# Two-layer hybrid encoder trunk: the recurrence's query and forget-gate projections computed in the product form, with the affine of the second layer's gates on ScalarE

## The chip, the cores and the metric

The kernel runs on one core of one Trainium2 chip. The metric is the device time of one execution in microseconds (us), the median over several runs. For the kernel before it is 1301.94 us (three runs, 1301.85 to 1302.33).

## The reference, cut to what matters

The program is two layers of an encoder on 256 tokens of width 1024, all in float32. Each layer projects the residual stream x once (`w_in`) and feeds three mixers with it: pooling, attention, and a bidirectional gated recurrence (HGRN2) with 8 heads of 128. The change touches only what goes into the recurrence:

```python
q = jax.nn.silu(heads(q_raw))                       # q_raw = x @ w_in[:, query columns]
def forget(raw, lb):                                # raw   = x @ w_in[:, gate columns], two directions
    z = heads(raw)
    f = lb + (1.0 - lb) * jax.nn.sigmoid(z)
    return (1.0 - lb) * jax.nn.sigmoid(-z), jnp.log(f)
```

`lb` is zero in layer 0 and one value per channel in layer 1. From f, (1-f) and q the recurrence forms running products over chunks of the tokens, then small matrix products. The three mixers are projected, gated and added, an output projection and a layer norm follow, then a SwiGLU FFN and a second layer norm.

## The kernel before, in words

All weights are streamed once, as 212 chunks of 1 MB. For each chunk a DMA brings `raw` (line 207), ScalarE rounds it to float32r, `whi` (line 225), and VectorE subtracts, `wlo` = raw - whi (line 228). x is kept in the same two parts, xh and xl, side by side in one tile `xx` (hi, then lo, 256 tokens each). A product is then hi*hi + hi*lo + lo*hi, three float32r products that add up to nearly float32. `raw`, `whi` and `wlo` have three buffers each.

There are three ways to multiply with a chunk:

- `gemm_cols` (lines 360 to 367): the chunk holds 256 output columns in 8 contraction tiles. For each of two halves m and each k there are three matmuls of 256 tokens (lines 356 to 358): whi*xh, whi*xl, wlo*xh, 48 matmuls per chunk. Both halves fit into one PSUM bank.
- `gemm_wide` (lines 369 to 381), the product form: for each m and k one matmul of whi with all 512 columns of `xx`, which gives hi*hi in the left half of a bank and hi*lo in the right half, and one matmul of wlo with xh, 32 matmuls per chunk. Each m needs a bank of its own, and the two halves of the bank must be added afterwards. `joined` (lines 383 to 387) does that: per m a copy of the left half by ScalarE (line 386), then VectorE adds the right half to it (line 387).
- `tok_part` (lines 398 to 408, matmuls at line 407), with tokens as output rows, in 24 matmuls per chunk.

The FFN, the pooling projection and three of the attention chunks use the product form already.

The work of one layer goes in this order: the recurrence's value chunks (v), then four head pairs, hp0 to hp3 here. Each head pair takes three chunks: the query (called q below), the forward gate (f0) and the backward gate (f1). Behind hp0 come four chunks for the output gate, behind hp1 four and behind hp3 two for attention's values. Then come the attention's query and key chunks and the rest.

The order on ScalarE, VectorE and TensorE is fixed while the program is written. At the end of each chunk's matmuls `step_end` (line 337) emits, in this order: the recurrence's "background" work on VectorE (scans, reciprocals, products, lines 524 to 577) up to a budget written in the code, then the eviction of the chunk just multiplied, and then `split_chunk`, which emits the `wlo` subtraction that the previous step left over and the `whi` of a new chunk. So when chunk n has been multiplied, the `wlo` that is emitted belongs to chunk n+2, and the `whi` to chunk n+3. Each engine runs its list in order.

The evictions before: for q, ScalarE takes the sigmoid from PSUM (line 935) and VectorE multiplies it with PSUM (line 936). For a gate chunk, ScalarE takes sigmoid(z) and sigmoid(-z) from PSUM (lines 945 and 948), and VectorE sets two border columns to 1 (line 946). In layer 1 four more VectorE instructions of 256 columns follow, the affine with `omlb` = 1-lb and `lb` (lines 952 and 954).

`gbank` hands out four PSUM banks in turn. A step of `gemm_cols` takes one, a step of `gemm_wide` two.

Of the kernel before, what the change touches and what calls it, by code (L numbers as in the profile page):

```python
# [11 lines left out]
AF = mybir.ActivationFunctionType  # L12
ALU = mybir.AluOpType
# [4 lines left out]
S = 256  # L18
# [60 lines left out]
def trunk(ctx: ExitStack, tc: tile.TileContext, x, p, w_in, pool_w, pool_scale, w_branch_a,  # L79
# [3 lines left out]
    V, A, PE, G = nc.vector, nc.scalar, nc.tensor, nc.gpsimd  # L83
# [39 lines left out]
    def gbank():  # L123
        return psg.tile([P, 512], F32, tag="g", name="g")
# [127 lines left out]
    def use_chunk():  # L252
        if pos["use"] == pos["split"] - 1:
            flush()
        i = pos["use"]
        pos["use"] += 1
        return split.pop(i)
# [79 lines left out]
    def step_end(then=None, budget=3000, banks=1, need=0, keep=2):  # L337


        background(budget)  # L340
        if then is not None:
            pend.append((then, banks, need))
        while pend:
            fn, _, n = pend[0]
            if held[0] + n > 10 and sum(e[1] for e in pend) <= keep:
                break
            pend.pop(0)
            if n:
                room(n)
            fn()  # L350
        split_chunk()
# [8 lines left out]
    def gemm_cols(w, act, ps, nk=8, m0=0, nm=2):  # L360
        for m in range(nm):
            if m == 1:
                amid()
            for k in range(nk):
                ms = slice((m0 + m) * P, (m0 + m + 1) * P)
                mm3(ps[:, m * S:(m + 1) * S], (w[0][:, k, ms], w[1][:, k, ms]),
                    act(k), k == 0, k == nk - 1)
# [15 lines left out]
    def joined(ps, dst):  # L383

        for m in range(2):
            A.activation(out=dst[:, m, :], in_=ps[m][:, 0:S], func=AF.Copy)  # L386
            V.tensor_tensor(out=dst[:, m, :], in0=dst[:, m, :], in1=ps[m][:, S:2 * S], op=ALU.add)  # L387
# [417 lines left out]
    lb = cst.tile([P, 16], F32, name="lb")  # L805
    omlb = cst.tile([P, 16], F32, name="omlb")
# [31 lines left out]
    for l in range(DEPTH):  # L838
# [6 lines left out]
        if l == 0:  # L845
# [9 lines left out]
            ps = [gbank(), gbank()]  # L855
# [37 lines left out]
        else:  # L893

            ws = [use_chunk() for _ in range(3)]
            ps = [[gbank(), gbank()] for _ in range(2)]
# [30 lines left out]
        vb = slot("s7", [P, 2, 512])  # L927
        for hp in range(4):
            five = []
            ps_q = gbank()  # L930
            gemm_cols(use_chunk(), xk, ps_q)

            def ev_q(ps=ps_q, five=five):
                q = half2k([P, 512])
                A.activation(out=q, in_=ps, func=AF.Sigmoid)
                V.tensor_tensor(out=q, in0=q, in1=ps, op=ALU.mult)
                five.append(q)
            step_end(ev_q, need=1)
            for d in range(2):
                ps = gbank()  # L940
                gemm_cols(use_chunk(), xk, ps)

                def ev_f(ps=ps, d=d, hp=hp, five=five):
                    ft, kt = half2k([P, 514]), half2k([P, 512])
                    A.activation(out=ft[:, 1:513], in_=ps, func=AF.Sigmoid)
                    V.tensor_scalar(out=ft[:, 0:514:513], in0=ft[:, 1:513:511], scalar1=1.0, scalar2=1.0,
                                    op0=ALU.max, op1=ALU.min)
                    A.activation(out=kt, in_=ps, func=AF.Sigmoid, scale=-1.0)
                    if l > 0:
                        for h in range(2):  # L950
                            i = 8 * d + 2 * hp + h
                            V.tensor_scalar(out=ft[:, 1 + h * S:1 + (h + 1) * S], in0=ft[:, 1 + h * S:1 + (h + 1) * S],
                                            scalar1=omlb[:, i:i + 1], scalar2=lb[:, i:i + 1], op0=ALU.mult, op1=ALU.add)
                            V.tensor_scalar(out=kt[:, h * S:(h + 1) * S], in0=kt[:, h * S:(h + 1) * S],
                                            scalar1=omlb[:, i:i + 1], scalar2=None, op0=ALU.mult)
                    five.extend((ft, kt))
                    if d == 1:
                        tasks.append(("hgrn", hgrn_task(l, hp, *five, vt, gt, oh, ol)))
                step_end(ev_f, need=2)
            if hp == 0:  # L960
                for hf in range(2):
                    def ev(t, ps, hf=hf):
                        s = misc([P, 512])
                        A.activation(out=s, in_=ps, func=AF.Sigmoid)
                        V.tensor_tensor(out=gt[:, t, 512 * hf:512 * hf + 512], in0=ps, in1=s, op=ALU.mult)
                        if hf == 1 and t == 1:
                            gated.add(l)
                    tok_block(xtok, ev)
            for g in {1: (0, 1), 3: (2,)}.get(hp, ()):
                def ev(t, ps, g=g):  # L970
                    dst = va[:, t, 512 * g:512 * g + 512] if g < 2 else vb[:, t, :]
                    A.activation(out=dst, in_=ps, func=AF.Copy)
                tok_block(xperm, ev)

        ob = slot("s8", [P, 2, 4, S], F32R)
        for jp in range(2):
            qk = []
            for i in range(6):
# [4 lines left out]
                else:  # L983
                    ps = gbank()
# [298 lines left out]
```

## Time and profile before

| | us |
|---|---|
| median of three runs | 1301.94 |
| the profiled execution's own time | 1301.92 |
| its span, first to last instruction | 1300.1 |
| TensorE matmul busy | 1285.5 |
| VectorE busy | 911.3 |
| ScalarE busy | 620.6 |
| GpSimd busy | 16.7 |

The clock granted to TensorE was 0.997 of full speed over the span. 1.82 us of the execution's time lie outside the span. In the rows of the profile PE is TensorE's matmul, PEld its weight load, DVE VectorE, ACT ScalarE. A row of a timeline begins with its start and its duration in us; in brackets stands the idle time in front of it and what ended it. A matmul's duration is longer than the distance to the next one, since matmuls are pipelined: the pace is read from the starts. A row of a group gives the number of instructions, the busy us and the mean ns of one.

### The profile page before, as it was taken

What the parts mean: (1) busy time and instruction counts of PE and PEld (TensorE: products, weight loads), DVE (VectorE), ACT (ScalarE), POOL (GpSimd) and SP (SyncE); (2) the same over time, 40 slices, a digit from 0 to 9 for tenths busy, and PEclk for the clock granted to TensorE, in tenths of its full rate; (3) what the DMA queues carried; (4) which work ended last, traced back from release to release, by engine and by line L of the source; (5) the groups of instructions that cost most, each with busy time, mean ns of one, the idle gap of its engine ahead of it and who ended that gap; (6) DMA issues with size and microseconds to landing.
All of it is one profiled execution on the core that took longest, in us unless ns stands there. A gap on an engine that the chain in (4) does not pass through costs nothing.

```text
span 1300.1 us, 18288 instructions
## 1 busy us (share of the span) xinstructions
PE 1285.5 (99%) x7663; PEld 1125.5 (87%) x7663; DVE 911.3 (70%) x1197; ACT 620.6 (48%) x742; POOL 16.7 (1%) x24
## 2 busy tenths in 40 slices
PE   9999999999999999999999999999999999999997
PEld 6999999888888788888888999999888887888885
DVE  5688798676556866665568988886955568666655
ACT  5444544654344455554254444445534435555531
POOL 0000000000000000000000000000000000000000
PEclk9999999999999999999999999999999999999998
DMA  9465545445555465557545544544445664566660
GB/s 321 162 195 162 163 163 161 133 132 195 200 193 194 162 196 188 181 184 265 185 162 186 173 161 162 175 151 147 145 164 201 207 220 157 169 188 193 213 240 33
DMA packets 160290, 233.32 MB, mean 179 GB/s; under 512 B 3856, under 2 KB 108880, under 8 KB 160208
## 3 DMA queue, kind: packets, MB, share of 16 engines
q1 hardware_dynamic: 158512, 227.44, 52.9%
q10 hardware_dynamic: 1696, 4.72, 1.1%
q8 instruction: 60, 0.98, 0.3%
q14 instruction: 22, 0.18, 0.0%
HBM read 231.10 MB, written 1.05 MB: 179 GB/s over the span
## 4 chain that ended last, share of the span: by engine, by line
PE 96%; DVE 2%; ACT 0%; DMA 0%; issue 0%; SPq 0%; DVEq 0%
PE g L407 33%; PE g L380 15%; PE g L356 11%; PE g L357 11%; PE g L358 11%; PE t L380 9%; DVE wlo L228 1%; PE t L589 1%; PE t L616 1%; PE t L644 1%; PE t L643 1%; PE t L723 1%; PE t L692 1%; PE t L446 0%; DMA raw<-in_w_in_dram 0%; PE t L671 0%
## 5 line engine op out<-in xcount | busy, mean ns | idle before, releaser
L228 DVE TENSOR_TENSOR wlo<-raw,whi 128x2048 fp32r<-128x2048 f32 (+1 forms) x220 | 487.7, 2224 | 88.5 <-ACT whi L225 88.4
L225 ACT ACTIVATE whi<-raw 128x2048 fp32r<-128x2048 f32 (+1 forms) x220 | 409.6, 1865 | 204.4 <-PE g L407 101.7
L407 PE MATMUL g<-whi,xx 128*128 128x512 f32 x960 | 293.5, 392 | 0.7 <-ACT whi L225 0.3
L407 PEld LDWEIGHTS g<-whi,xx 128*128 128x128 f32 x960 | 179.2, 189 | 37.9 <-ACT whi L225 1.7
L380 PE MATMUL g<-xx,whi 128*128 128x512 f32 x576 | 202.7, 397 | 0.0
L356 PE MATMUL g<-xx,whi 128*128 128x256 f32 x672 | 191.6, 285 | 0.0
L358 PE MATMUL g<-xx,wlo 128*128 128x256 f32 x672 | 190.1, 283 | 0.0
L357 PE MATMUL g<-xx,whi 128*128 128x256 f32 x672 | 190.1, 283 | 0.0
L407 PE MATMUL g<-wlo,xx 128*128 128x512 f32 x480 | 182.2, 392 | 2.6 <-DVE wlo L228 2.3
L380 PE MATMUL g<-xx,wlo 128*128 128x256 f32 x576 | 148.9, 279 | 0.0
L356 PEld LDWEIGHTS g<-xx,whi 128*128 128x128 f32 x672 | 128.8, 192 | 0.6
L357 PEld LDWEIGHTS g<-xx,whi 128*128 128x128 f32 x672 | 128.9, 192 | 0.3
L358 PEld LDWEIGHTS g<-xx,wlo 128*128 128x128 f32 x672 | 128.8, 192 | 0.0
L380 PE MATMUL t<-xx,whi 128*128 128x512 f32 x352 | 123.6, 396 | 0.0
L380 PEld LDWEIGHTS g<-xx,whi 128*128 128x128 f32 x576 | 105.4, 188 | 19.5
L380 PEld LDWEIGHTS g<-xx,wlo 128*128 128x128 f32 x576 | 108.6, 189 | 5.8
L407 PEld LDWEIGHTS g<-wlo,xx 128*128 128x128 f32 x480 | 90.6, 189 | 24.7 <-DVE wlo L228 6.1
L380 PE MATMUL t<-xx,wlo 128*128 128x256 f32 x352 | 90.9, 279 | 0.0
L380 PEld LDWEIGHTS t<-xx,whi 128*128 128x128 f32 x352 | 64.5, 188 | 11.9
L380 PEld LDWEIGHTS t<-xx,wlo 128*128 128x128 f32 x352 | 66.3, 188 | 3.9
L407 PE MATMUL g<-whi,s 128*128 128x512 f32 x192 | 59.1, 389 | 0.0
L387 DVE TENSOR_TENSOR m<-m,t 128x256 f32<-128x256 f32 x44 | 18.5, 421 | 56.1 <-ACT m L386 56.1
(194 smaller groups left out, 1635.3 us busy)
## 6 DMA issues: line engine op xcount, KB each, us to landing
raw<-in_w_in_dram SPq DMA_DIRECT2D x106, 1024.0 KB, 5.1
raw<-in_w_ffn_gate_dram SPq DMA_DIRECT2D x22, 1024.0 KB, 5.3
raw<-in_w_ffn_up_dram SPq DMA_DIRECT2D x22, 1024.0 KB, 5.4
raw<-in_w_ffn_down_dram SPq DMA_DIRECT2D x22, 1024.0 KB, 5.0
raw<-in_w_branch_c_dram SPq DMA_DIRECT2D x8, 1024.0 KB, 5.2
raw<-in_w_branch_a_dram SPq DMA_DIRECT2D x8, 1024.0 KB, 5.8
raw<-in_w_out_dram SPq DMA_DIRECT2D x8, 1024.0 KB, 5.0
raw<-in_w_ple_gate_dram SPq DMA_DIRECT2D x8, 1024.0 KB, 5.1
```

Of the source, the lines that this page charges most:

```text
L225: A.activation(out=hi[:, ks, :], in_=t[:, ks, :], func=AF.Copy)
L228: V.tensor_tensor(out=lo[:, ks, :], in0=t[:, ks, :], in1=f(hi[:, ks, :]), op=ALU.subtract)
L356: PE.matmul(ps, lhsT=ah, rhs=bh, start=first, stop=False)
L357: PE.matmul(ps, lhsT=ah, rhs=bl, start=False, stop=False)
L358: PE.matmul(ps, lhsT=al, rhs=bh, start=False, stop=last)
L380: PE.matmul(o, lhsT=a, rhs=b, start=k == 0 and i == 0, stop=k == KD - 1 and i == 1, skip_group_check=True)
L387: V.tensor_tensor(out=dst[:, m, :], in0=dst[:, m, :], in1=ps[m][:, S:2 * S], op=ALU.add)
L407: PE.matmul(ps, lhsT=a, rhs=b, start=i == 0 and k == 0 and p == 0, stop=i == n - 1 and k == 3 and p == 2)
L589: PE.matmul(dgs[0][po:po + 64, co:co + 64], lhsT=KI[:, cs], rhs=QI[:, cs], start=True, stop=True)
L616: PE.matmul(lg[:, co:co + P], lhsT=kp.rearrange("p b u -> p (b u)"), rhs=qp.rearrange("p b u -> p (b u)"), start=True, stop=True)
L643: PE.matmul(o, lhsT=at[:, 2 * h + t, :], rhs=vt[:, t, hs], start=True, stop=False)
L644: PE.matmul(o, lhsT=al[:, 2 * h + 1 - t, :], rhs=vt[:, 1 - t, hs], start=False, stop=True)
```

## The change

The q, f0 and f1 chunks of all four head pairs (12 per layer, 24 in all) are multiplied with `gemm_wide` and joined by `joined`. After that, ScalarE works on the joined tile in SBUF: one SiLU for q, and for a gate first sigmoid(-z), then sigmoid(z) in place. In layer 1 the affine goes from VectorE to ScalarE, four activations of 256 columns with a per-channel scale (and bias). The product of line 936 is gone. `step_end` is told that two banks are held.

```diff
-            ps_q = gbank()
-            gemm_cols(use_chunk(), xk, ps_q)
+            ps_q = [gbank(), gbank()]
+            gemm_wide(use_chunk(), ps_q)
 
             def ev_q(ps=ps_q, five=five):
                 q = half2k([P, 512])
-                A.activation(out=q, in_=ps, func=AF.Sigmoid)
-                V.tensor_tensor(out=q, in0=q, in1=ps, op=ALU.mult)
+                joined(ps, q.rearrange("p (m t) -> p m t", t=S))
+                A.activation(out=q, in_=q, func=AF.Silu)
                 five.append(q)
-            step_end(ev_q, need=1)
+            step_end(ev_q, banks=2, need=1)
             for d in range(2):
-                ps = gbank()
-                gemm_cols(use_chunk(), xk, ps)
+                ps = [gbank(), gbank()]
+                gemm_wide(use_chunk(), ps)
 
                 def ev_f(ps=ps, d=d, hp=hp, five=five):
                     ft, kt = half2k([P, 514]), half2k([P, 512])
-                    A.activation(out=ft[:, 1:513], in_=ps, func=AF.Sigmoid)
+                    joined(ps, ft[:, 1:513].rearrange("p (m t) -> p m t", t=S))
+                    A.activation(out=kt, in_=ft[:, 1:513], func=AF.Sigmoid, scale=-1.0)
+                    A.activation(out=ft[:, 1:513], in_=ft[:, 1:513], func=AF.Sigmoid)
                     V.tensor_scalar(out=ft[:, 0:514:513], in0=ft[:, 1:513:511], scalar1=1.0, scalar2=1.0,
                                     op0=ALU.max, op1=ALU.min)
-                    A.activation(out=kt, in_=ps, func=AF.Sigmoid, scale=-1.0)
                     if l > 0:
                         for h in range(2):
                             i = 8 * d + 2 * hp + h
-                            V.tensor_scalar(out=ft[:, 1 + h * S:1 + (h + 1) * S], in0=ft[:, 1 + h * S:1 + (h + 1) * S],
-                                            scalar1=omlb[:, i:i + 1], scalar2=lb[:, i:i + 1], op0=ALU.mult, op1=ALU.add)
-                            V.tensor_scalar(out=kt[:, h * S:(h + 1) * S], in0=kt[:, h * S:(h + 1) * S],
-                                            scalar1=omlb[:, i:i + 1], scalar2=None, op0=ALU.mult)
+                            fs, ks = slice(1 + h * S, 1 + (h + 1) * S), slice(h * S, (h + 1) * S)
+                            A.activation(out=ft[:, fs], in_=ft[:, fs], func=AF.Identity,
+                                         scale=omlb[:, i:i + 1], bias=lb[:, i:i + 1])
+                            A.activation(out=kt[:, ks], in_=kt[:, ks], func=AF.Copy, scale=omlb[:, i:i + 1])
...
-                step_end(ev_f, need=2)
+                step_end(ev_f, banks=2, need=2)
```

The order of the steps, of the background work and of the splits is the same as before on every engine; what changes is what stands inside an eviction. On VectorE, in layer 0, this is the end of the f1 step of hp2 before: background products (lines 541 to 567, on work tiles w), the border columns (946), and the wlo of the chunk two steps on (228).

```order
L228 TENSOR_TENSOR wlo<-raw,whi 128x2048
L541 TENSOR_TENSOR w<-h,w 128x8x32
L542 TENSOR_TENSOR w<-h,w 128x8x32
L544 TENSOR_TENSOR w<-h,w 128x8x32
L545 TENSOR_TENSOR w<-h,w 128x8x32
L550 COPY tot<-w 128x16
L565 TENSOR_TENSOR w<-h,w 128x2x3x32
L567 TENSOR_TENSOR w<-w,tot 128x2x3x32
L565 TENSOR_TENSOR w<-h,w 128x2x3x32
L567 TENSOR_TENSOR w<-w,tot 128x2x3x32
L946 TENSOR_SCALAR h<-h 128x2
L228 TENSOR_TENSOR wlo<-raw,whi 128x2048
```

The same place on VectorE in the changed kernel, where the border columns have become line 948:

```order
L541 TENSOR_TENSOR w<-h,w 128x8x32
L542 TENSOR_TENSOR w<-h,w 128x8x32
L544 TENSOR_TENSOR w<-h,w 128x8x32
L545 TENSOR_TENSOR w<-h,w 128x8x32
L550 COPY tot<-w 128x16
L565 TENSOR_TENSOR w<-h,w 128x2x3x32
L567 TENSOR_TENSOR w<-w,tot 128x2x3x32
L565 TENSOR_TENSOR w<-h,w 128x2x3x32
L567 TENSOR_TENSOR w<-w,tot 128x2x3x32
L387 TENSOR_TENSOR h<-h,g 128x256 x2
L948 TENSOR_SCALAR h<-h 128x2
L228 TENSOR_TENSOR wlo<-raw,whi 128x2048
```

The two additions stand between the background work and the border columns, and the `wlo` stands behind all of them. The border columns read the result of sigmoid(z), which ScalarE writes after both additions.

On ScalarE, in layer 1, these are the evictions of f0 and f1 of hp2 before, each with the `whi` behind it (line 225):

```order
L945 ACTIVATE h<-g 128x512
L948 ACTIVATE h<-g 128x512
L225 ACTIVATE whi<-raw 128x2048
L945 ACTIVATE h<-g 128x512
L948 ACTIVATE h<-g 128x512
L225 ACTIVATE whi<-raw 128x2048
```

And f0 alone in the changed kernel, from the copies out of PSUM (386) over the two sigmoids (946, 947) and the affine (954, 956) to the same `whi`:

```order
L386 ACTIVATE h<-g 128x256 x2
L946 ACT_TABLE_LOAD
L946 ACTIVATE h<-h 128x512
L947 ACTIVATE h<-h 128x512
L954 ACTIVATE h<-h,lb,omlb 128x256
L956 ACTIVATE h<-h,omlb 128x256
L954 ACTIVATE h<-h,lb,omlb 128x256
L956 ACTIVATE h<-h,omlb 128x256
L225 ACTIVATE whi<-raw 128x2048
```

An eviction of two instructions has become one of eight in f0. The table load is there because SiLU and sigmoid stand in different tables: the whole program had 7 such loads and has 20.

## The prediction

> **What bounds the kernel now.** I read the page first: the span, the engines, and the chain that ended last.
>
> ```profile
> span 1300.1 us, 18288 instructions
> PE 1285.5 (99%) x7663; PEld 1125.5 (87%) x7663; DVE 911.3 (70%) x1197; ACT 620.6 (48%) x742; POOL 16.7 (1%) x24
> PE 96%; DVE 2%; ACT 0%; DMA 0%; issue 0%; SPq 0%; DVEq 0%
> ```
>
> TensorE is busy for 99% of the span and is 96% of the chain. So a microsecond less of its work shows in the end, and so does a microsecond in which it waits. My sum is made against the profiled execution's 1301.92 us (the span and 1.82 us outside it), which is the median of the runs shown (1301.94) within 0.02. About 0.2%, 2.6 us, is what a measurement of this kernel can tell from no change.
>
> Next the waits of TensorE, and the engines' busy time in the two recurrence stretches (layer 0, layer 1) and in a stretch of the FFN, where the product form already runs.
>
> ```profile
> PE g L407 <- DVE wlo L228: 2.3, 2, 1.2
> ```
>
> ```profile
> 31.40:162.00 130.60, 130.60 (x949) 120.81 (x949) 100.22 (x147) 63.79 (x77) 2.04 (x2) 1.00 0.53 172
> 673.00:803.60 130.60, 130.60 (x950) 120.80 (x949) 108.03 (x166) 63.73 (x76) 2.03 (x2) 1.00 0.52 170
> 471.50:594.00 122.50, 122.50 (x696) 106.51 (x695) 80.60 (x87) 68.97 (x88) 0.00 (x0) 1.00 0.61 195
> ```
>
> Columns: length, then PE, PEld, DVE, ACT, POOL busy. The recurrence stretches have no gap on TensorE, but VectorE is busy for 77% and 83% of them, against 66% in the FFN, and it works in long unbroken runs. What the change does to VectorE's order there decides.
>
> **Term 1, TensorE: a gain.** First and last rows of a run of three old chunks, then of three product-form chunks in the FFN:
>
> ```profile
> 31.65 0.28 PE L357 MATMUL g<-xx,whi 128*128 128x256 f32 x1
> ...
> 48.69 0.28 PE L358 MATMUL g<-xx,wlo 128*128 128x256 f32 x1
> ```
>
> ```profile
> 471.46 0.39 PE L380 MATMUL t<-xx,whi 128*128 128x512 f32 x1
> ...
> 488.24 0.39 PE L380 MATMUL g<-xx,whi 128*128 128x512 f32 x1
> ```
>
> 142 starts in 17.04 us are 0.120 each, so 48 matmuls take 5.76 us. Three product chunks in 16.78 us are 5.59 each. 24 chunks by 0.167 us give 4.0 us. TensorE alone would make it 1301.9 - 4.0 = 1297.9 us. A third fewer matmuls save only 3%, since a matmul of 512 columns takes about twice as long.
>
> **Term 2, the eviction: a longer ladder between two engines.** Rows of the FFN's join and SiLU (ScalarE, then VectorE), and two PSUM additions with the split behind them:
>
> ```profile
> 482.85 0.38 ACT L386 ACTIVATE m<-g 128x256 f32<-128x256 f32 x1 [1.29 <-PE g L380]
> 483.72 0.63 ACT L1216 ACTIVATE m<-m 128x512 f32<-128x512 f32 x1 [0.49 <-DVE m L387]
> ```
>
> ```profile
> 483.27 0.42 DVE L387 TENSOR_TENSOR m<-m,g 128x256 f32<-128x256 f32 x1 [0.52 <-ACT m L386]
> ...
> 248.75 0.75 DVE L996 SCALAR_TENSOR_TENSOR h<-g,h 128x256 f32<-128x256 f32 x2
> 249.42 2.28 DVE L228 TENSOR_TENSOR wlo<-raw,whi 128x2048 fp32r<-128x2048 f32 x1
> ```
>
> A handover costs 0.04 (482.85 + 0.38 to 483.27), two additions 0.75, an activation of 512 columns from SBUF 0.63. Now VectorE and TensorE around f0 and f1 of hp2, layer 0; the PE rows are the first matmuls of f1, of q of hp3 and of its f0:
>
> ```profile
> 128.74 0.11 DVE L946 TENSOR_SCALAR h<-h 128x2 f32<-128x2 f32 x1
> 128.75 2.29 DVE L228 TENSOR_TENSOR wlo<-raw,whi 128x2048 fp32r<-128x2048 f32 x1
> 130.95 0.42 DVE L541 TENSOR_TENSOR w<-h,w 128x256 f32<-128x256 f32 x1
> ...
> 133.19 0.35 DVE L567 TENSOR_TENSOR w<-w,tot 128x192 f32<-128x192 f32 x1
> 134.33 0.17 DVE L946 TENSOR_SCALAR h<-h 128x2 f32<-128x2 f32 x1 [0.80 <-ACT h L945]
> 134.41 2.29 DVE L228 TENSOR_TENSOR wlo<-raw,whi 128x2048 fp32r<-128x2048 f32 x1
> ```
>
> ```profile
> 127.74 0.28 PE L356 MATMUL g<-xx,whi 128*128 128x256 f32 x1
> 133.50 0.28 PE L356 MATMUL g<-xx,whi 128*128 128x256 f32 x1
> 139.26 0.28 PE L356 MATMUL g<-xx,whi 128*128 128x256 f32 x1
> ```
>
> Before, once VectorE reaches a gate's eviction the next `wlo` is done 0.08 + 2.29 = 2.37 us later. After: two additions 0.75, handover, sigmoid(-z) 0.63, handover, sigmoid(z) 0.63, handover, border columns 0.08, split 2.29, in all 4.5 us. VectorE stands still for 1.4 us of it, and everything queued behind it is 2.1 us later. The `wlo` of f1 of hp2 was done at 136.7 and is wanted at 139.5 (f0 of hp3 begins at 139.26, its first `wlo` matmul 0.24 behind): 2.8 us to spare. After: f0's eviction starts at 128.7 as before, its `wlo` ends at 133.2, the background work (130.95 to 133.5) ends at 135.6, f1's `wlo` ends at 140.1. TensorE, four converted steps (0.67 us) ahead and 0.1 us late from the chunk before, wants it at 138.9. It waits 1.2 us.
>
> In layer 1 the affine leaves VectorE, so this ladder grows by less:
>
> ```profile
> L952 DVE TENSOR_SCALAR h<-h,omlb,lb 128x256 f32<-128x256 f32 x16 | 6.6, 413 | 0.3
> L954 DVE TENSOR_SCALAR h<-h,omlb 128x256 f32<-128x256 f32 x16 | 5.6, 347 | 0.0
> L427 ACT ACTIVATE sa<-t,vec 128x256 fp32r<-128x256 f32 x16 | 7.6, 475 | 15.1 <-PE t L671 11.7 <-DVE sb L428 3.3
> ```
>
> At that place 1.3 us (four of these, overlapped) go out of VectorE's queue and the ladder is only 0.9 longer. But the four come onto ScalarE ahead of the next `whi` at about 0.4 each (line 427, with one per-channel operand, is the nearest row; bounds are 0.35, as on VectorE, and 0.63, an activation of twice the columns, which moves each late place of layer 1 by some 0.5 us either way). The Trainium skill, "ScalarE: Activation LUTs", section "Rules for kernel authors", gives multiplies and adds to VectorE, not ScalarE; the rows above agree (347 to 413 ns there, 475 ns here). So ScalarE's chain in an f0 step is: 0.2 until the second copy starts, 0.38, table load 1.28, sigmoids and handovers 1.4, border columns 0.2, affine 1.6, `whi` 1.8: 6.9 us in a step of 5.6. f1's copies start 1.3 us late, and its `wlo` about 1.1 us later than before.
>
> **Term 3, the table loads.**
>
> ```profile
> 237.81 1.28 ACT L708 ACT_TABLE_LOAD   x1
> 239.10 0.72 ACT L708 ACTIVATE m<-m,nm 128x512 f32<-128x512 f32 x1
> ```
>
> A load takes 1.28 us, and the activation follows it at once. 13 more are 16.7 us on an engine that is 48% busy; they wait for nothing, and run while VectorE is late with the additions. Where it is not late (f0 of hp0) a load costs 0.8 us of slack. The Trainium skill, "ScalarE: Activation LUTs", "What ACT_TABLE_LOAD costs", counts a drain with each switch, 2.66 us in all; here no gap stands beside the load, so I go by 1.28.
>
> **Term 4, where the lateness reaches TensorE.** Two more places where little was to spare, layer 1: the third output-gate chunk and f0 of hp1 (each time the `wlo` and the matmul that first uses it).
>
> ```profile
> 698.87 2.23 DVE L228 TENSOR_TENSOR wlo<-raw,whi 128x2048 fp32r<-128x2048 f32 x1
> ...
> 716.50 2.28 DVE L228 TENSOR_TENSOR wlo<-raw,whi 128x2048 fp32r<-128x2048 f32 x1
> ```
>
> ```profile
> 701.77 0.39 PE L407 MATMUL g<-wlo,xx 128*128 128x512 f32 x1
> ...
> 718.99 0.28 PE L358 MATMUL g<-xx,wlo 128*128 128x256 f32 x1
> ```
>
> To spare: 0.67 and 0.21 us. Both are in one unbroken VectorE run that starts 1.1 us later. Against a TensorE that is 0.2 us ahead at the first, it waits 0.7; at the second 0.4, being late by then itself. And behind f1 of hp3, where the recurrence's normalisation (lines 648, 650) waits behind that eviction on ScalarE:
>
> ```profile
> 799.39 0.28 ACT L648 ACTIVATE m<-t 128x128 f32<-128x128 f32 x1 [1.76 <-PE t L644]
> 800.57 0.17 DVE L650 TENSOR_SCALAR ms<-ms 128x4 f32<-128x4 f32 x1 [1.10 <-ACT m L648]
> 804.43 2.28 DVE L228 TENSOR_TENSOR wlo<-raw,whi 128x2048 fp32r<-128x2048 f32 x1
> 807.75 0.28 PE L358 MATMUL g<-xx,wlo 128*128 128x256 f32 x1
> ```
>
> VectorE reaches that eviction about 3.5 us after TensorE ended the chunk; the ladder, affine and `whi` add 5.8, so line 650 comes at 10.5 us instead of 6.0 (the chunk ended at 794.5), the `wlo` 4.4 us late. It had 1.0 to spare and TensorE is 0.9 late by then: 2.5 us.
>
> All places, by the same sums with their own rows. Layer 0: f0 of hp1 0.3, the value chunk behind it 0.4, q of hp3 0.1, f0 of hp3 1.2, the first attention chunk 0.1: 2.1 us. Layer 1: three output-gate chunks 0.3, 0.7, 0.2; f0 of hp1 0.4, the value chunk 0.5, q of hp3 0.2, f0 of hp3 1.2, the value chunk behind hp3 0.9, the first attention chunk 2.5: 6.9 us. Apart from the rows shown these are estimates. Sum: -4.0 + 2.1 + 6.9 = +5.0, so 1306.9 us.
>
> What costs nothing: PSUM. A step holds two of four banks, so step n's additions must end before step n+2 starts; the latest end 4.3 us behind TensorE, and 5.6 are to be had. Without that cover its price would be the excess. A `raw` load that starts 3 us later (5.1 us to land) is still there when its `whi` comes three steps on.
>
> **The rivals.**
>
> *The splits keep up.* The ladder is shorter than I make it (sigmoids overlap, additions slip in ahead), and TensorE never waits: 1297.9 us, faster. For it: 48% and 70% busy, and TensorE hardly waits today. Against it: the queues are in order, and the slack of 0.2 to 2.8 us stands in rows. It decides if VectorE's standstill is under about 0.3 us instead of 1.4.
>
> *Gain and stalls cancel.* Only the 1.2 us places and the two short ones of layer 1 are real, and the normalisation isn't delayed, because ScalarE does the affine faster: stalls of 3 to 5 us, 1301 to 1303 us, no change.
>
> *ScalarE becomes the bound.* If a table switch empties the engine and so costs its own 1.28 us a second time, the eight f0 evictions are each 0.5 to 1.3 us later, by how late VectorE is already: some 5 us beyond the forecast, 1312 us. Against it: the row shows the activation right behind the load. The Trainium skill, "ScalarE: Activation LUTs", "What ACT_TABLE_LOAD costs", would have it so, with its drain of about 1.38 us.
>
> **How the numbers follow.** Forecast of stalls in the 6 to 11 us class (1304.5 to 1309.5): 0.52. Splits keep up: 0.18. Cancel: 0.20. ScalarE bound: 0.10. The range takes the first rival's end at one side, 1297.8, and the last's at the other, 1312. Faster by over 0.2%: 0.19; within: 0.22; slower: 0.59.
>
> **What would show it.** Starts of product-form chunks 5.59 us apart where nothing waits; line 228 as releaser of lines 380 and 407 in TensorE's waits, about 9 us in all, two thirds of it in layer 1; line 948 waiting some 1.4 us for line 947; f0 of hp3 late by about 1.2 us in both layers, the first attention chunk of layer 1 by 2.5. If TensorE waits under 2 us, my ladder is wrong; if it waits for banks, PSUM is what I missed; if gaps stand around the table loads, the third rival holds.

## The result, and the profile after

| | us |
|---|---|
| before, median of 4 runs (range) | 1301.89 (1301.54 to 1302.33) |
| after, median of 4 runs (range) | 1308.73 (1307.83 to 1309.40) |
| ratio after to before, 95% interval | 1.0053 (1.0040 to 1.0065) |
| after, the profiled execution, and its span | 1309.39, 1307.5 |

The changed kernel is 0.5% slower. Its four runs are two pairs, 1307.83 and 1308.07, and 1309.39 and 1309.40; the profiled one is of the upper pair. What parts the pairs is told below, at the first attention chunk and in the last section.

The page of the kernel after, the same three lines as before (span, engines, chain):

```profile
span 1307.5 us, 17602 instructions
PE 1286.6 (98%) x7279; PEld 1105.1 (85%) x7279; DVE 913.2 (70%) x1205; ACT 669.6 (51%) x835; POOL 16.7 (1%) x24
PE 85%; DVE 10%; ACT 3%; issue 1%; POOL 0%; DVEq 0%; POOLq 0%
```

TensorE has 384 matmuls fewer. VectorE's busy time is the same within 2 us. But 10% of the chain that ended last is now VectorE's and 3% ScalarE's: work of these two has come between TensorE's matmuls. The waits of TensorE in the kernel after (total, times, longest) name it:

```profile
PE g L407 <- DVE wlo L228: 4.3, 7, 1.2
PE g L358 <- DVE wlo L228: 2.3, 1, 2.3
PE g L380 <- DVE wlo L228: 2.0, 2, 1.0
```

8.6 us for low parts (`wlo`) in place of 2.3. And VectorE's group of border-column instructions, in the kernel before and in the kernel after (busy, mean ns, idle time in front of it):

```profile
L946 DVE TENSOR_SCALAR h<-h 128x2 f32<-128x2 f32 x16 | 2.4, 152 | 17.8 <-ACT h L945 17.8
```

```profile
L948 DVE TENSOR_SCALAR h<-h 128x2 f32<-128x2 f32 x16 | 2.7, 170 | 23.5 <-ACT h L947 23.5
```

In the kernel after, VectorE stands still at each of the 16 gates, 23.5 / 16 = 1.47 us in the mean, until ScalarE has done sigmoid(z). The 17.8 us of before are of another kind: they lie at nine gates, where VectorE had come early and waited for the chunk's end and its sigmoid, and at the other seven, where it came late, there was no wait at all. Now it waits 1.36 us or more also where it is late already.

The stretches of the kernel after: the first two are those of the recurrence as before, the third has no counterpart. The column behind the five engines is the granted clock:

```profile
31.40:162.00 130.60, 129.31 (x755) 109.43 (x756) 104.98 (x161) 81.70 (x108) 2.04 (x2) 1.00 0.50 165
673.00:803.60 130.60, 127.81 (x745) 107.12 (x744) 101.24 (x145) 89.18 (x126) 1.01 (x1) 1.00 0.50 164
814.00:820.00 6.00, 6.00 (x52) 5.80 (x51) 4.90 (x9) 0.47 (x1) 0.00 (x0) 0.77 0.63 185
```

TensorE had no gap in either recurrence stretch before; now 1.3 us are missing in layer 0 and 2.8 in layer 1 by busy time (a matmul's row is longer than the distance to the next start, so the gaps read from the starts are larger). VectorE is busy for 5 us more in layer 0 and 7 less in layer 1, ScalarE for 18 and 25 us more.

The place on which the prediction's ladder was worked out, f0 and f1 of hp2 in layer 0, on VectorE of the kernel after:

```profile
128.56 0.69 DVE L387 TENSOR_TENSOR h<-h,g 128x256 f32<-128x256 f32 x2
130.61 0.17 DVE L948 TENSOR_SCALAR h<-h 128x2 f32<-128x2 f32 x1 [1.36 <-ACT h L947]
130.69 2.29 DVE L228 TENSOR_TENSOR wlo<-raw,whi 128x2048 fp32r<-128x2048 f32 x1
...
135.39 0.75 DVE L387 TENSOR_TENSOR h<-h,g 128x256 f32<-128x256 f32 x2
137.50 0.17 DVE L948 TENSOR_SCALAR h<-h 128x2 f32<-128x2 f32 x1 [1.36 <-ACT h L947]
137.58 2.29 DVE L228 TENSOR_TENSOR wlo<-raw,whi 128x2048 fp32r<-128x2048 f32 x1
```

From the first addition to the end of the `wlo` it takes 130.69 + 2.29 - 128.56 = 4.42 us, 1.36 of it standing still. The `wlo` of f1 is done at 139.87. TensorE, f0 of hp3, in the kernel after:

```profile
138.31 0.63 PE L380 MATMUL g<-xx,whi 128*128 128x512 f32 x2
139.92 0.50 PE L380 MATMUL g<-xx,wlo 128*128 128x256 f32 x2 [0.98 <-DVE wlo L228]
```

The `wlo` matmul starts 0.05 after the split's end. The second matmul of the first row started at 138.54, so the distance is 1.38; behind a matmul of 512 columns 0.23 is usual: a stall of 1.15 us.

### The profile page after: what moved, and what is told of

It is laid out like the page before. It is cut to its first block, busy times and chain, and to the rows that moved or that the text cites. A ratio compares the mean times of both kernels' runs of the same rounds, so it can differ in the third digit from the quotient of the medians.

```text
span 1307.5 us, 17602 instructions
## 1 busy us (share of the span) xinstructions
PE 1286.6 (98%) x7279; PEld 1105.1 (85%) x7279; DVE 913.2 (70%) x1205; ACT 669.6 (51%) x835; POOL 16.7 (1%) x24
## 4 chain that ended last, share of the span: by engine, by line
PE 85%; DVE 10%; ACT 3%; issue 1%; POOL 0%; DVEq 0%; POOLq 0%
PE g L407 29%; PE g L380 19%; PE t L380 9%; PE g L358 7%; PE g L357 7%; PE g L356 7%; DVE wlo L228 4%; DVE h L387 1%; DVE w L539 1%; PE t L616 1%; PE t L446 1%; ACT h L947 1%; ACT h L946 1%; PE t L723 1%; PE t L692 1%
## 5 line engine op out<-in xcount | busy, mean ns | idle before, releaser
L380 PE MATMUL g<-xx,whi 128*128 128x512 f32 x960 | 336.8, 397 | 0.0
L380 PE MATMUL g<-xx,wlo 128*128 128x256 f32 x960 | 248.8, 280 | 2.1 <-DVE wlo L228 2.0
L380 PEld LDWEIGHTS g<-xx,whi 128*128 128x128 f32 x960 | 175.0, 188 | 33.0
L358 PE MATMUL g<-xx,wlo 128*128 128x256 f32 x288 | 82.4, 286 | 2.4 <-DVE wlo L228 2.3
L356 PE MATMUL g<-xx,whi 128*128 128x256 f32 x288 | 82.7, 287 | 0.0
L357 PE MATMUL g<-xx,whi 128*128 128x256 f32 x288 | 82.0, 285 | 0.0
L356 PEld LDWEIGHTS g<-xx,whi 128*128 128x128 f32 x288 | 55.9, 194 | 0.1
L357 PEld LDWEIGHTS g<-xx,whi 128*128 128x128 f32 x288 | 55.9, 194 | 0.1
```

Of the source, the lines that this page charges most:

```text
L356: PE.matmul(ps, lhsT=ah, rhs=bh, start=first, stop=False)
L357: PE.matmul(ps, lhsT=ah, rhs=bl, start=False, stop=False)
L358: PE.matmul(ps, lhsT=al, rhs=bh, start=False, stop=last)
L380: PE.matmul(o, lhsT=a, rhs=b, start=k == 0 and i == 0, stop=k == KD - 1 and i == 1, skip_group_check=True)
```

## What ScalarE's part does in layer 1

ScalarE behind f0 and f1 of hp3, layer 1, kernel after: affine of f0, `whi`, then affine of f1, `whi`, then the normalisation's squares (648).

```profile
796.06 0.60 ACT L954 ACTIVATE h<-h,lb,omlb 128x256 f32<-128x256 f32 x1 [0.24 <-DVE h L948]
796.57 0.49 ACT L956 ACTIVATE h<-h,omlb 128x256 f32<-128x256 f32 x1
...
797.86 1.91 ACT L225 ACTIVATE whi<-raw 128x2048 fp32r<-128x2048 f32 x1
...
804.52 1.90 ACT L225 ACTIVATE whi<-raw 128x2048 fp32r<-128x2048 f32 x1
806.32 0.25 ACT L648 ACTIVATE m<-t 128x128 f32<-128x128 f32 x1
```

The four activations take 797.86 - 796.06 = 1.8 us a gate. The Trainium skill, "ScalarE: Activation LUTs", section "What ACT_TABLE_LOAD costs", adds some 93 ns for each per-channel operand; the rows agree (0.60 with scale and bias, 0.49 with scale alone). The squares could start at 799.39 before and start at 806.32 now. VectorE waits for them (650), and the `wlo` of the first attention chunk stands behind it:

```profile
807.46 0.17 DVE L650 TENSOR_SCALAR ms<-ms 128x4 f32<-128x4 f32 x1 [2.58 <-ACT m L648]
...
811.31 2.28 DVE L228 TENSOR_TENSOR wlo<-raw,whi 128x2048 fp32r<-128x2048 f32 x1
```

TensorE at that chunk:

```profile
811.02 0.28 PE L357 MATMUL g<-xx,whi 128*128 128x256 f32 x1
813.64 0.58 PE L358 MATMUL g<-xx,wlo 128*128 128x256 f32 x1 [2.35 <-DVE wlo L228]
814.02 0.42 PE L356 MATMUL g<-xx,whi 128*128 128x256 f32 x1
...
816.59 0.35 PE L356 MATMUL g<-xx,whi 128*128 128x256 f32 x1
```

The stall is 813.64 - 811.02 - 0.12 = 2.5 us. Behind it twelve starts take 816.59 - 814.02 = 2.57 us, 0.214 each in place of the usual 0.120. The trace also keeps a record of the granted clock: it stands at half from 813.30 on, for 3.41 us, and the matmuls in that time lose 1.4 us. Nothing in the prediction had that.

All stalls, read from the distances between TensorE's starts. Layer 0: f0 of hp1 0.17, the value chunk behind it 0.46, f0 of hp3 1.15, the first attention chunk 0.17, in all 1.95 us. Layer 1: the second and the third output-gate chunk 0.47 and 0.6, f0 of hp1 0.2, the value chunk 0.45, f0 of hp3 1.2, the value chunk behind hp3 0.84, the first attention chunk 2.5, in all 6.3 us, and the clock's 1.4.

## The experiments

Beside each median stands its range. The kernel before ran on the same chip each time (medians 1301.93, 1301.85, 1301.63, 1301.89). Where a layer's share is named, it is the distance in the trace from TensorE's transposition that ends layer 0 to the second of the two 1.2 us waits that the kernel before has too: 438.3 us before, 445.1 after.

**e4: the matmuls alone.** Only the left half of each bank is evicted, for q and the gates, with the instructions of the kernel before in two halves; hi*lo is computed and left out. For q:

```diff
-                joined(ps, q.rearrange("p (m t) -> p m t", t=S))
-                A.activation(out=q, in_=q, func=AF.Silu)
+                for m in range(2):
+                    A.activation(out=q[:, m * S:(m + 1) * S], in_=ps[m][:, 0:S], func=AF.Sigmoid)
+                for m in range(2):
+                    V.tensor_tensor(out=q[:, m * S:(m + 1) * S], in0=q[:, m * S:(m + 1) * S], in1=ps[m][:, 0:S], op=ALU.mult)
```

> The product form's matmuls with the evictions of the kernel before, two instructions of 256 columns for each of 512, reading the left half of each bank only: the hi*lo term is computed and left out of the result, there is no join, the sigmoid's product and the affine are on VectorE. It measures TensorE's gain by itself. My theory: no new wait, 1297 to 1299 us. Rival (the product form doesn't reach 5.59 us per chunk between the recurrence's small matmuls, or two banks per step are too few): 1300 to 1304 us.

Measured: 1297.85 us (1297.64 to 1298.69), ratio to before 0.9970 (0.9959 to 0.9982). The waits of TensorE are those of before:

```profile
PE g L407 <- DVE wlo L228: 2.3, 2, 1.2
PE t L852 <- DVE w L848: 1.5, 1, 1.5
```

So the product form alone is worth the 4.0 us, and all that is lost is lost in the evictions. Layer 1 takes 436.5 us, 8.7 less than in the changed kernel: the 6.3 us of stalls, the clock's 1.4, and 1.0 in gaps too short to list.

**e2: one table fewer.** q gets the sigmoid only, its product with z is left out; the program has 7 table loads again.

```diff
-                A.activation(out=q, in_=q, func=AF.Silu)
+                A.activation(out=q, in_=q, func=AF.Sigmoid)
```

> The changed kernel with sigmoid in place of SiLU for q (the product by z is left out), so that 13 table loads of 1.28 us go from ScalarE and nothing else moves. My theory: most loads run while VectorE is late, only f0 of hp0 gains and with it the start of layer 1's long VectorE run: 1.5 to 3 us less than the changed kernel, 1305 to 1307.5 us. Rival (ScalarE and its loads bound the stretch): the stalls go, 1298 to 1301 us.

Measured: 1308.31 us (1307.63 to 1308.45), ratio 1.0049 (1.0036 to 1.0061). By the medians that is 0.4 us for 13 loads, within the spread of the runs, so both numbers were missed. Between the two profiled executions, which both have the clock at half behind the first attention chunk, it is 1.0 us (1309.39 and 1308.36). The starts say where: in layer 1 the stall at the second output-gate chunk is gone and the third's is 0.4 us instead of 0.6, which fits the effect through f0 of hp0 that was expected, only smaller. The other stalls stand where they stood (the first attention chunk 2.5 us). In the kernel after, each load starts 0.02 us behind the activation before it. Of the 15 loads in front of a q or a gate, four are followed by the next activation after 0.01 us; behind the other eleven it starts 0.05 to 1.46 us later, when VectorE's additions (line 387) are done, and there the load costs nothing.

**e3: the affine back on VectorE,** inside the same eviction, behind the border columns.

```diff
-                            A.activation(out=ft[:, fs], in_=ft[:, fs], func=AF.Identity,
-                                         scale=omlb[:, i:i + 1], bias=lb[:, i:i + 1])
-                            A.activation(out=kt[:, ks], in_=kt[:, ks], func=AF.Copy, scale=omlb[:, i:i + 1])
+                            V.tensor_scalar(out=ft[:, fs], in0=ft[:, fs], scalar1=omlb[:, i:i + 1],
+                                            scalar2=lb[:, i:i + 1], op0=ALU.mult, op1=ALU.add)
+                            V.tensor_scalar(out=kt[:, ks], in0=kt[:, ks], scalar1=omlb[:, i:i + 1],
+                                            scalar2=None, op0=ALU.mult)
```

> The changed kernel with layer 1's affine on VectorE, behind the border columns, as in the kernel before. My theory: VectorE's ladder grows by 1.25 us per gate in layer 1, ScalarE is 1.6 us freer, so the wait at the first attention chunk (and with it any drop of the clock) becomes small, and those at f0 of hp3 and the value chunks grow: 1306 to 1312 us. Rival (the affine on ScalarE is what costs): all of layer 1's 6.5 us of stalls go down to layer 0's 2 us, 1300 to 1304 us.

Measured: 1312.62 us (1311.77 to 1313.11), ratio 1.0083 (1.0069 to 1.0096), just above the expected range and far from the rival's; layer 1 takes 447.2. By the starts the first attention chunk's stall falls to 0.6 us (the chain over line 648 is shorter), but others grow or come, the largest 2.5 us at f1 of hp3 and 1.7 instead of 0.45 at the value chunk behind f0 and f1 of hp1. Given the join, moving the affine to ScalarE paid by about 4 us.

**e1: the borders filled ahead of the join,** so that they need no sigmoid.

```diff
                     ft, kt = half2k([P, 514]), half2k([P, 512])
+                    V.memset(ft[:, 0:514:513], 1.0)
                     joined(ps, ft[:, 1:513].rearrange("p (m t) -> p m t", t=S))
...
-                    V.tensor_scalar(out=ft[:, 0:514:513], in0=ft[:, 1:513:511], scalar1=1.0, scalar2=1.0,
-                                    op0=ALU.max, op1=ALU.min)
```

> The changed kernel, but the two border columns of a gate are set by a memset ahead of the join, which reads nothing, instead of by an instruction that reads sigmoid(z). My theory (VectorE stands still for ScalarE's two sigmoids, and the weight splits queue behind it): the ladder from the additions to the next wlo falls from 4.5 to about 3.0 us, layer 0 loses its 2.0 us of stalls, layer 1 loses its output-gate, f0 and value-chunk stalls, but the 2.5 us wait at the first attention chunk stays, since ScalarE's affine still holds up the normalisation: 1300 to 1303 us. Rival (the added work and the table loads themselves are too much): within 2 us of the changed kernel, 1307 to 1310 us.

Measured: 1305.67 us (1305.16 to 1307.09), ratio 1.0032 (1.0020 to 1.0045): neither. Layer 0 has no stall left, layer 1 three, of 0.4, 1.2 and 4.05 us. The trace shows a new wait that the edit brought, ScalarE's copies of a gate in layer 1:

```profile
767.63 0.66 ACT L386 ACTIVATE h<-g 128x256 f32<-128x256 f32 x2 [3.11 <-DVE h L945]
...
789.47 0.66 ACT L386 ACTIVATE h<-g 128x256 f32<-128x256 f32 x2 [3.16 <-DVE h L945]
```

The fill stands behind VectorE's background work, and the copies, which write the same tile, wait for it. The fill belongs behind the additions.

**e5: the fill behind the additions.**

```diff
                     joined(ps, ft[:, 1:513].rearrange("p (m t) -> p m t", t=S))
+                    V.memset(ft[:, 0:514:513], 1.0)
                     A.activation(out=kt, in_=ft[:, 1:513], func=AF.Sigmoid, scale=-1.0)
                     A.activation(out=ft[:, 1:513], in_=ft[:, 1:513], func=AF.Sigmoid)
-                    V.tensor_scalar(out=ft[:, 0:514:513], in0=ft[:, 1:513:511], scalar1=1.0, scalar2=1.0,
-                                    op0=ALU.max, op1=ALU.min)
```

> The borders of the gate tile are written as ones by a fill directly behind the join's two additions, instead of being made from the sigmoid's result behind both sigmoids; nothing of VectorE then waits for ScalarE inside a gate's eviction, and no copy on ScalarE waits for the fill. Theory (VectorE's wait of about 1.4 us for the two sigmoids makes the next low part late): layer 0 keeps no stall (2.0 us less than the changed kernel's 1308.7), layer 1 keeps the stalls that ScalarE's affine makes by standing ahead of the normalisation of the value path, above all 2 to 3 us ahead of the first attention chunk, so 1301 to 1304 us. Rival (the low parts are late because of the work itself, three ladders of additions, copies and splits, and not because of the wait): 1306 to 1309 us.

Measured: 1303.83 us (1301.91 to 1304.75, 11 runs), ratio 1.0013 (1.0004 to 1.0022). The theory holds: the time is in its range, layer 0 has no stall, and layer 1 keeps the one ahead of the first attention chunk. f0 and f1 of hp2 in layer 0, on VectorE of e5:

```profile
127.17 0.68 DVE L387 TENSOR_TENSOR h<-h,g 128x256 f32<-128x256 f32 x2
127.90 2.29 DVE L228 TENSOR_TENSOR wlo<-raw,whi 128x2048 fp32r<-128x2048 f32 x1
...
132.60 0.75 DVE L387 TENSOR_TENSOR h<-h,g 128x256 f32<-128x256 f32 x2
133.39 2.28 DVE L228 TENSOR_TENSOR wlo<-raw,whi 128x2048 fp32r<-128x2048 f32 x1
```

Addition to end of `wlo` now 3.0 us, nothing stands still, and the second `wlo` is done at 135.67 instead of 139.87 (f0's additions are 1.4 earlier here). VectorE's busy time is 912.6 against 913.2. Of the waits of TensorE in e5, one is new against before:

```profile
PE g L358 <- DVE wlo L228: 3.3, 1, 3.3
```

It is the first attention chunk of layer 1, behind the normalisation, for which VectorE waits here too:

```profile
801.16 0.17 DVE L650 TENSOR_SCALAR ms<-ms 128x4 f32<-128x4 f32 x1 [3.92 <-ACT m L648]
```

**e7: the affine behind the `whi`.** As e5, with layer 1's affine kept in a list that is emitted after `split_chunk`.

```diff
         split_chunk()
+        while behind:
+            behind.pop(0)()
```

> As the fill behind the additions, and the affine stays on ScalarE but is issued behind the copy that makes the next high part. Theory (what is late in layer 1 is the normalisation of the value path, which still stands behind the affine): within 1 us of the kernel with the fill alone, 1301 to 1304 us. Rival (what is late is the next high part, and with it the low part): 1300 us or less.

Measured: 1303.23 us (1301.03 to 1304.02), ratio 1.0008 (0.9999 to 1.0017), 0.6 from e5. The wait ahead of the first attention chunk is 2.9 us instead of 3.3. So it isn't the late `whi` that costs.

**e10: the last pair as before.** As e5, but f0 and f1 of hp3 in layer 1 go back to `gemm_cols` and the old eviction.

```diff
-                ps = [gbank(), gbank()]
-                gemm_wide(use_chunk(), ps)
+                wide = l == 0 or hp < 3
+                if wide:
+                    ps = [gbank(), gbank()]
+                    gemm_wide(use_chunk(), ps)
+                else:
+                    ps = gbank()
+                    gemm_cols(use_chunk(), xk, ps)
```

> As the fill behind the additions; of layer 1 only the last pair's two forget-gate chunks go back to the way of the kernel before, the other three pairs' keep the product form with the affine on ScalarE inside the eviction. Theory (what is left in layer 1 is one place, the normalisation of the value path behind the last pair's affine): 22 of 24 chunks keep their gain (3.7 us) and no stall is left, 1298 to 1299.5 us. Rival (the lateness is gathered over all four pairs): the wait ahead of the first attention chunk or of the value chunk behind the last pair stays, over 1300.5 us.

Measured: 1299.27 us (1298.79 to 1299.80, 11 runs), ratio 0.9981 (0.9972 to 0.9990). The wait of 3.3 us is gone with this one place; of the others the value chunk behind hp3 keeps 0.4 us. Layer 1 takes 437.5 us.

**e8: layer 1's gates as before.** As e5, with `wide = l == 0`.

> As the fill behind the additions; in layer 1 the forget-gate chunks go back to the way of the kernel before (matmul form, both sigmoids out of PSUM, affine on VectorE) and only the query chunks keep the product form. Theory: 16 of the 24 chunks keep their gain of 0.167 us (12 query and gate chunks of layer 0, 4 query chunks of layer 1, 2.7 us), with no stall but those of the kernel before: 1298.5 to 1300.5 us. Rival (the query chunks themselves make the splits late in layer 1, or layer 0's gates do even without the wait): over 1301 us.

Measured: 1299.27 us (1299.08 to 1299.39, 11 runs), ratio 0.9980 (0.9972 to 0.9989), with the waits of the kernel before and no others. Layer 1 takes 437.8 us. The six gate chunks that e10 has more should be worth 1.0 us and bring 0.2 there; 0.5 of it are its two small stalls, the rest wasn't traced. Both are faster than the kernel before, e10 by 2.4 us and e8 by 2.6, the fastest with the whole computation in them; e8 is the simpler one.

**e6 and e9: the affine moved into the recurrence.** As e5, with the affine as the first piece of each direction's background work, on VectorE (e6) or on ScalarE (e9). The edit of e9 is shown; e6 has the two VectorE instructions of e3 in this place and `yield 1250`, the number by which the budget counts the piece:

```diff
             f0 = ft[:, 1:513]
+            if l > 0:
+                for h in range(2):
+                    i = 8 * d + 2 * hp + h
+                    fs, ks = slice(1 + h * S, 1 + (h + 1) * S), slice(h * S, (h + 1) * S)
+                    A.activation(out=ft[:, fs], in_=ft[:, fs], func=AF.Identity,
+                                 scale=omlb[:, i:i + 1], bias=lb[:, i:i + 1])
+                    A.activation(out=kt[:, ks], in_=kt[:, ks], func=AF.Copy, scale=omlb[:, i:i + 1])
+                yield 300
```

> As the fill behind the additions, and layer 1's gate affine taken off ScalarE's eviction and put on VectorE as the first piece of each direction's recurrence, among its background work. Theory (the two waits, for the sigmoids in layer 0 and for the affine in layer 1, are all that the change adds beside its 4 us of matmul time): no stall in either layer, 1298.5 to 1301 us, below the kernel before. Rival (VectorE has no room for 32 more affine operations of about 0.33 us among the background of layer 1, and the splits fall behind there): 1302 to 1306 us.

> As the fill behind the additions, and layer 1's gate affine stays on ScalarE but is issued as the first piece of each direction's recurrence instead of inside the gate's eviction. Theory (the affine's 1.8 us a gate costs by standing ahead of the next high part and of the normalisation of the value path, and ScalarE has the time elsewhere): the 3.3 us wait ahead of the first attention chunk goes and no other comes, all 24 chunks keep their gain, 1297.8 to 1299.5 us. Rival (VectorE's scans then wait for ScalarE, whose queue holds copies that wait for matmuls, and the next low parts stand behind the scans): 1301 to 1306 us, with waits for low parts in layer 1's attention chunks, as when VectorE took the affine there.

Measured: e6 1307.39 us (1307.26 to 1308.28), e9 1307.88 us (1307.48 to 1308.29), ratios 1.0045 (1.0033 to 1.0058) and 1.0047 (1.0034 to 1.0061). Both are above even their rivals' ranges, and both have the same new waits in the attention part, near 870, 893 and 957 us (e9 one more of 0.7 near 700); the wait ahead of the first attention chunk is gone in both. VectorE of e9, and behind it the same work in e5, where the line numbers are eight lower:

```profile
861.87 1.21 DVE L540 TENSOR_TENSOR_SCAN w<-h,kc 128x512 f32<-128x512 f32 x1
...
869.03 0.49 DVE L583 TENSOR_TENSOR w<-w,t 128x128 f32<-128x128 f32 x2
869.44 2.28 DVE L228 TENSOR_TENSOR wlo<-raw,whi 128x2048 fp32r<-128x2048 f32 x1
```

```profile
862.01 1.70 DVE L539 RECIPROCAL w<-w 128x256 f32<-128x256 f32 x1
863.62 2.23 DVE L228 TENSOR_TENSOR wlo<-raw,whi 128x2048 fp32r<-128x2048 f32 x1
865.77 0.41 DVE L541 TENSOR_TENSOR w<-h,w 128x256 f32<-128x256 f32 x1
```

In e9 7.6 us of one recurrence (scan to products) stand in one piece ahead of a `wlo`; in e5 a `wlo` stands between its reciprocals and its products. With the affine as a background piece the other pieces fall into other steps, the last pair's into one lump; e6 has the same lump. That the two engines give the same time speaks against VectorE's load and against waits for ScalarE, the two rivals' mechanisms. Which rule of the emission makes the lump wasn't tried apart.

**e11 and e12: one wait elsewhere.** On e8, one low part is computed three or four times over (`again`), to see what the clock does behind a wait that has nothing to do with the change. The edit of e11, without the lines that issue the next load only once; e12 has 4 and 105 in place of 3 and 111:

```diff
-        return lambda: lo_part(slice(0, k))
+        again = 3 if pos["split"] == 111 else 1
+
+        def low():
+            for _ in range(again):
+                lo_part(slice(0, k))
+        return low
```

> The kernel with only layer 1's gate chunks as before (1299.27 us, its 11 runs within 0.3 us), with one low part near the end of layer 0's MLP (at about 619 us, where VectorE does nothing but splits and TensorE takes each low part 1.1 us after it is done) computed three times over: 2 x 2.29 us more, so TensorE waits there once for about 3.5 us, far from all that the change touches. Theory (a wait of TensorE that takes most of a 3.41 us stretch is followed by a stretch of half the granted clock, and this, not the change, makes the extra 1.4 to 1.7 us): the clock record shows half for 3.41 us or 6.83 us behind the wait, and the time is 1304.0 to 1305.0 us, 3.5 for the wait and 1.4 to 1.7 for the clock, at least in some of the runs. Rival (the fall of the clock belongs to the work of layer 1's recurrence, a wait of TensorE costs its own length): 1302.8 us in all runs, and no half clock in the record.

> The kernel with only layer 1's gate chunks as before (1299.27 us), with one low part in the last matmuls of layer 0's MLP (near 622 us, where VectorE does nothing but splits and TensorE takes each low part 1.1 us after it is done) computed four times over: 3 x 2.29 us more, so one wait of TensorE of about 5.8 us, too long to lie across two stretches of 3.41 us without emptying most of one, and far from all that the change touches. Theory (a stretch of 3.41 us that TensorE mostly waits through is followed by one at half the granted clock): half the clock for 3.41 or 6.83 us behind the wait in the profile's record, in all runs, and 1306.3 to 1308.5 us, 5.8 for the wait and 1.4 to 3.4 for the clock. Rival (the wait costs its own length and the clock stays): 1305.0 us and no half clock in the record.

Measured: e11 1302.34 us (1301.83 to 1303.89, 11 runs), e12 1300.00 us (1299.16 to 1300.47). Neither made the wait it was meant to make. In e11 the repeats fell among the value chunks of layer 1, where TensorE waited once:

```profile
668.76 0.50 PE L414 MATMUL g<-wlo,xx 128*128 128x512 f32 x1 [2.19 <-DVE wlo L229]
```

In this profiled execution (1302.12 us) the clock stayed. But the eleven runs are two groups, seven from 1301.83 to 1302.72 and four from 1303.32 to 1303.89, where e8's are within 0.3. The mean granted clock of the runs is 0.997 or 0.998 in the first group and 0.996 or 0.997 in the second; 3.41 us at half are 0.0013 of it. That fits a halved clock in the four, but none of these was profiled, so it isn't shown. In e12 there was more to spare than I took from the rows, TensorE waited 0.2 us, and nothing follows from it.

## Why the prediction was right, point by point

**Term 1, the matmuls: right.** 1297.9 predicted for TensorE alone, 1297.85 measured (e4).

**Term 2, the ladder: right in mechanism and size.** 4.5 us predicted from addition to `wlo`, 4.42 measured; standstill 1.4 against 1.36; f1's `wlo` at 140.1 against 139.87; f0 of hp3 waits 1.2 against 1.15. e5 shows that the standstill is what costs and not the work: with the wait gone and the work left, layer 0 has no stall and layer 1 a single one of over 0.2 us. For layer 1 one reading in this step was off: it laid the 1.1 us by which VectorE's run with the output-gate chunks and f0 of hp1 starts late on ScalarE's chain of copies, load and affine. That chain is still there in e5, while those stalls are not: by itself it makes none. With the standstill it counts for something, as in e2, where the stall at the second output-gate chunk goes with the load. Without the standstill, what is left of the affine's cost stands at the normalisation. Its size, 1.6 us a gate, was 1.8.

**Term 3, the table loads: right.** They were put down as nearly hidden, and e2 puts 13 of them at 0.4 us by the medians and 1.0 between profiled executions. The rival that a switch empties the engine and costs its 1.28 us a second time, some 5 us in all, falls with it, and so do the gaps that it needs: the rows show 0.02 us ahead of a load.

**Term 4, the places: right but for small ones.** Layer 0 2.1 predicted, 1.95 measured; layer 1 6.9 against 6.3 and the 1.0 in short gaps, the largest (2.5, 1.2, 0.84) at the places named and within 0.1 of the sums. Of the three output-gate places (0.3, 0.7, 0.2) two had a stall, the second chunk's 0.47 and the third's, whose rows the prediction shows, 0.6 instead of 0.7; q of hp3 had none in either layer. PSUM cost nothing, as said: no bank stands among TensorE's waits.

**What the sum lacked: the clock.** The wait ahead of the first attention chunk was priced at its length. In the profiled execution it also halved the granted clock for 3.41 us, 1.4 us more. By its time and its mean clock one more of the four runs had the same (0.996 in the upper pair, 0.998 in the lower). That is the step between the two pairs, 1307.95 and 1309.40 in the mean. Without it the forecast was 1.0 us low. By the traces, layer 1 without the clock is 5.5 us longer than before, where the sum had 4.9: its matmuls gain 1.8 instead of 2.0 (e4), and the lateness is 7.3 instead of 6.9. Layer 0 is 0.5 longer instead of 0.1, but its share holds the start of the program, and the kernels without a stall there (e4, e5, e8, e10) reach one and the same matmul of its attention part between 370.8 and 371.9 us, so that isn't told from scatter.

**One slip in the classes.** Stalls of 6 to 11 us on top of 1297.9 are 1303.9 to 1308.9, and not the 1304.5 to 1309.5 that stand beside them. The result, 1308.73, lies in both.

## What to carry to other kernels

When an eviction is handed from engine to engine, look for the last small instruction that reads back what the other engine wrote: everything queued behind it waits for the whole ladder, and a constant needs no such reading. Put it where its own queue has just passed and where nobody waits for it; the same fill a few instructions earlier only moved the wait to the other engine. A saving on the bounding engine is worth making stage by stage: here 16 of 24 chunks gave 2.6 us, six more nothing that could be measured, and the last two cost more than all the others saved.

## What the runs showed that I had not expected

A single wait of TensorE of 2.35 us was enough for half the clock over the next 3.41 us, in two of the four runs (one of them by its time and mean clock alone). By the profiled executions: the longest waits of after, e2, e7, e9, e5 and e1, from 2.35 to 3.9 us, were followed by 3.41 us at half, the 4.3 us of e6 by 6.83; the waits of 2.3 us in e3 and 2.19 in e11 were not.

The clock record of after stands at full speed for 805.55 us before it falls, which is 236 times 3.413; in e5, e7, e6 and e9 it is 235, 234, 253 and 254 times. So it is judged in fixed stretches of 3.41 us. Three pairs of such stretches follow, from after, e1 and e3: length, then the busy time of the engines, TensorE's matmuls first, and third from the end the granted clock.

```profile
809.89:813.30 3.41, 1.41 (x8) 1.00 (x6) 3.41 (x8) 2.20 (x2) 0.00 (x0) 1.00 0.01 2
813.30:816.72 3.42, 3.08 (x14) 3.08 (x15) 3.38 (x10) 0.20 (x1) 0.00 (x0) 0.50 0.58 159
```

```profile
804.16:807.58 3.42, 1.76 (x9) 1.31 (x7) 2.48 (x12) 3.42 (x4) 0.80 (x1) 1.00 0.01 2
807.58:810.99 3.41, 1.17 (x9) 1.18 (x10) 3.38 (x7) 0.59 (x1) 0.00 (x0) 1.00 0.02 3
```

```profile
784.52:787.93 3.41, 1.87 (x11) 1.26 (x9) 2.90 (x6) 3.39 (x5) 0.00 (x0) 1.00 0.06 21
787.93:791.35 3.42, 2.63 (x15) 2.25 (x15) 3.39 (x7) 2.06 (x3) 0.00 (x0) 1.00 0.41 117
```

The long wait of e1 lies across two stretches. Behind the first of them, with 1.76 us of matmuls, the clock stays; behind the second, with 1.17, it falls (at 810.99). The wait of e3 is as long as that of after, but lies across two stretches with 1.87 and 2.63 us of matmuls, and nothing follows. All profiled executions fit one limit: the clock fell behind every stretch with 1.55 us of matmuls or less (e9 has the 1.55), and behind none with 1.75 or more. So what decides is how much of a wait lies in one stretch, and that can differ from run to run: of e5's eleven runs four take 1301.91 to 1302.53 us with a mean clock of 0.998, and seven take 1303.36 to 1304.75 with 0.996 or 0.997. One thing is left open: e6's clock stayed low through a stretch that had 1.99 us of matmuls at half speed. The Trainium skill, "TensorE: Matmul & The Clock Gate", section "What's actually happening", has the same window, free-running, and lets the clock fall after an idle one; the length agrees, but here a window with 1.55 us of matmuls in it was enough.
